# Attention units in three stages one unit apart, with TensorE's order as written, in a two-layer diffusion backbone

## The chip, the core and the metric

The kernel runs on one core of a Trainium2 chip. The core has a matrix engine, TensorE (PE in the rows, with its weight loads as PEld), VectorE (DVE), ScalarE (ACT), GpSimd (POOL) and SyncE (SP), which here mostly issues DMAs. Each engine works through its own queue in order, and engines wait for each other by semaphores. The metric is the device time of one execution in microseconds (us), the median of several runs.

## The reference

Two layers run over 1024 latent tokens (a grid 64 wide) and 256 context tokens, with a width of 1024. A layer projects its input once and gives the columns to three mixers, an mLSTM, a neighbourhood attention and an RG-LRU. Their outputs are concatenated, go through one output projection and are added to the stream; a normed, gated MLP follows. The change concerns the neighbourhood attention and the output projection, which the reference writes so:

```python
q_r = lax.dynamic_index_in_dim(qg, r, axis=1, keepdims=False)
k_band = lax.dynamic_slice_in_dim(kg, sr, wr, axis=1)
...
s_loc = jnp.einsum('bqhd,brqchd->bhqrc', q_r, k_win).astype(jnp.float32) * scale
...
s_loc = (s_loc + bias.astype(jnp.float32)).reshape(b_, NA_HEADS, GRID_W, wr * wc)
s_ctx = jnp.einsum('bqhd,bkhd->bhqk', q_r, kc).astype(jnp.float32) * scale
p = jax.nn.softmax(jnp.concatenate([s_loc, s_ctx], axis=-1), axis=-1).astype(v.dtype)
...
o = jnp.einsum('bhqrc,brqchd->bqhd', p_loc, v_win) + jnp.einsum('bhqk,bkhd->bqhd', p_ctx, vc)
...
x = x + g1[:, None] * (jnp.concatenate([ym, yn, yl], axis=-1) @ w_out)
```

There are 8 heads of 64 columns. A latent token reads a window of 8 by 16 neighbours and all the context; a context token (in layer 0 only) reads the context.

## The kernel before

**Units.** Attention is done in head pairs (`hp`, four of them), and in each pair in units of 128 query tokens: 8 units over latent tokens in either layer, and in layer 0 two over context tokens ahead of them, 40 and 32 units in all. A unit has three parts. *Scores*: QS (the queries) times KH and KL (the keys' high and low part in the matmul's short format) for both heads `e`, into three banks `psa` of PSUM (one for a context unit). VectorE then adds a bias table and takes the maximum (two operations a head), and ScalarE takes the exponential into S and sums the rows into `den`. *Transposes*: S is transposed by TensorE in three groups, called T1, T2 and T3 here (four blocks of the first head, four of the second, and the last block of both); ScalarE copies T1 and T3 and VectorE T2 into PT. *Values*: `den` is inverted, spread to 128 columns as `rb` and transposed into bank `psc`, where PT times the values VB (window) and VC (context) is accumulated too. The result goes to `yr`, scaled by the inverse.

**Prep.** The stacks QS, KH and KL of a head pair are made by `na_prep`, in 6 steps (layer 0) or 5 (layer 1). A step loads `ut`, scales it by VectorE and transposes it into a bank; then for each of the two heads ScalarE copies the high part (KH or QS) and VectorE subtracts it to give the low part (KL or `ql`). The prep of the next head pair runs among the units of this one, a step at a unit's side.

**Fill.** Half of the output projection (its first four row blocks) is done during attention too: chains of 12 matmuls in the one bank `psp`, each with its own read of the stream `xs` and write back, 24 chains in layer 0 and 16 in layer 1. `side()` is called in every unit between scores and transposes; it issues the next prep step and as many chains as are due.

**Banks.** `psa` has three banks, `psb` two, and `psc`, `psp` and `psq` one each. Prep steps (of head pairs 1 to 3) and the three groups of transposes take theirs in the turn b, b, q:

```python
t = bank("bbq")
```

**Order.** The kernel is built with a scheduler that goes over each engine's instructions with a timeline of its own and sets the order of each queue. So the order in which the code issues units, prep steps and chains is not the order on the engines; waits between tiles are kept. Pools give out buffers in turn, so that a tile with `bufs=1` can be loaded again only when its last reader is done.

The functions that the change touches stand here, with the line numbers that the rows use.

Of the kernel before, what the change touches and what calls it, by code (L numbers as in the profile page):

```python
# [11 lines left out]
F32 = mybir.dt.float32  # L12
# [9 lines left out]
P = 128  # L22
# [3 lines left out]
NCTX = 256  # L26
# [65 lines left out]
def backbone_kernel(ctx: ExitStack, tc: tile.TileContext, I, out, dbg=None):  # L92
    nc = tc.nc
    dbg = dbg if dbg is not None else {}
    pe, dve, act, pool, sp = nc.tensor, nc.vector, nc.scalar, nc.gpsimd, nc.sync
# [519 lines left out]
    for l in range(DEPTH):  # L615
# [99 lines left out]
        def softmax_pv(npl, S, den, tiles, vals, permT, ydst):  # L715
# [7 lines left out]
            for gi, gr in enumerate(groups):  # L723
# [37 lines left out]
        anchors = []  # L761

        def new_den():
            return sm.tile([P, 2], F32, name=nm("den"), tag="den", bufs=4)
        def na_att(hp, npl, stacks, yr, side):
# [3 lines left out]
            VC = npl.tile([P, 2, P], F32, name=nm("VC"), tag="VC", bufs=1)  # L769
            uv = u_nv[l]  # L770
            sp.dma_start(VC, uv[0:NCTX, hp * P:(hp + 1) * P].rearrange("(t p) c -> p t c", p=P))

            if not last:
                for qt in range(2):
                    tS = bank("a")
                    S = []
                    den = new_den()
                    for e in range(2):
                        for i, K_ in enumerate((KH, KL)):
                            anchor = pe.matmul(tS[:, e * 256:(e + 1) * 256], QS[e][:, qt * P:(qt + 1) * P],  # L780
                                               K_[e][:, 0:256], start=(i == 0), stop=(i == 1))
                    anchors.append(anchor.ins)
                    for e in range(2):
                        s_ = npl.tile([P, 640], F32, name=nm("S"), tag="S", bufs=4)
                        nmx = sm.tile([P, 1], F32, name=nm("nmx"), tag="nmx", bufs=4)
                        mx = sm.tile([P, 1], F32, name=nm("mx"), tag="mx", bufs=4)
                        sv = tS[:, e * 256:(e + 1) * 256]
                        dve.tensor_reduce(mx, sv, axis=AX.X, op=OP.max)
                        dve.tensor_scalar(nmx, mx, -1.0, None, op0=OP.mult)
                        act.activation(s_[:, :256], sv, AF.Exp, bias=nmx, accum_out=den[:, e:e + 1])  # L790
                        S.append(s_)
# [5 lines left out]
                    side()  # L797
                    phase(f"na_att{l}")
                    softmax_pv(npl, S, den, [(0, P), (P, P)], [VC[:, 0], VC[:, 1]], ident, yd)


            for ct, bs in enumerate(((0,), (1, 2), (3,))):
# [10 lines left out]
                for b in bs:  # L813
                    VB = npl.tile([P, 4, P], F32, name=nm("VB"), tag="VB", bufs=3)
# [6 lines left out]
                    for g in range(2):  # L821
                        nr = 11 if g == 0 else 12
                        nl = nr * 32
                        r0 = 0 if g == 0 else 4
                        kc = (0, 8, 24, 32)[b]
                        qo = NCTX + (1 - g) * 512 + (3 - b) * P
                        tC = bank("a")
                        tL = []
                        for e in range(2):
                            tl = bank("a")  # L830
                            tL.append(tl)
                            for i, K_ in enumerate((KH, KL)):
                                kv = K_[e][:, NCTX:].rearrange("p (r c) -> p r c", c=64)[:, r0:r0 + nr, kc:kc + 32]
                                pe.matmul(tl[:, :nl].rearrange("p (r c) -> p r c", c=32), QS[e][:, qo:qo + P], kv,  # L834
                                          start=(i == 0), stop=(i == 1))
                        for e in range(2):
                            for i, K_ in enumerate((KH, KL)):
                                anchor = pe.matmul(tC[:, e * 256:(e + 1) * 256], QS[e][:, qo:qo + P],
                                                   K_[e][:, 0:256], start=(i == 0), stop=(i == 1))
                        anchors.append(anchor.ins)  # L840
                        S = []
                        den = new_den()
                        for e in range(2):

                            s_ = npl.tile([P, 640], F32, name=nm("S"), tag="S", bufs=4)
                            m1_ = sm.tile([P, 1], F32, name=nm("m1"), tag="m1", bufs=4)
                            m2_ = sm.tile([P, 1], F32, name=nm("m2"), tag="m2", bufs=4)
                            dve.tensor_tensor_reduce(out=s_[:, 0:nl], in0=tL[e][:, :nl],
                                                     in1=tab[e][:, 1 - g, 0:nl],
# [745 lines left out]
```

## Time and profile before

| What | Time |
|---|---|
| median of 3 runs | 3132.05 us (3132.0 to 3132.32) |
| profiled execution | 3124.27 us |
| its span, first to last instruction | 3122.5 us |
| TensorE busy in the span | 3020.2 us, 97% |
| VectorE busy | 1900.0 us, 61% |
| ScalarE busy | 1128.4 us, 36% |
| chain that ended last | PE 70%, DVE 11%, DMA 10% |

All rows come from one profiled execution, 7.8 us below the runs' median. Busy shares count instructions in flight on an engine. The chain that ended last is followed back from the last instruction, at each step to what released it; its shares say on which engine that chain's time was spent. Attention lies at about 510 to 760 us (layer 0) and 2129 to 2350 us (layer 1), with some matmuls of the stage behind it among the last units.

### The profile page before, as it was taken

How to read it: one execution, taken by the hardware profiler on the slowest of the kernel's cores; microseconds unless marked ns; L12 is line 12 of the kernel's file. 1: busy time of each engine (PE TensorE's matmuls, PEld its weight loads, DVE VectorE, ACT ScalarE, POOL GpSimd, SP SyncE). 2: the span in 40 equal slices, each digit the busy share in tenths (PEclk: the TensorE clock that was granted, in tenths of full speed). 3: DMA queues.
4: the chain of work that ended last, by engine and by line, in shares of the span. 5: the costliest groups of instructions: out<-in, count | busy, mean ns of one | idle time of the engine just before them, and what ended most of it. 6: DMA issues, size and time to landing. Idle time of an engine off the chain costs nothing.

```text
span 3122.5 us, 47474 instructions
## 1 busy us (share of the span) xinstructions
PE 3020.2 (97%) x18250; PEld 2558.1 (82%) x18250; DVE 1900.0 (61%) x4318; ACT 1128.4 (36%) x2011; POOL 291.0 (9%) x252
## 2 busy tenths in 40 slices
PE   7999998999899999999999999998899999999999
PEld 6888898778788888887778889997787777887877
DVE  5757655787977667455444574765787444444444
ACT  4632223574421222233222453234564222332222
POOL 0410000222200000010000511002222000000000
PEclk8999999999999999999999999999999999999999
DMA  9624567765233444233323632347753332333233
GB/s 272 216 73 144 171 190 199 226 169 178 68 115 105 126 124 125 75 108 101 95 88 94 175 123 82 100 131 219 219 172 110 95 95 89 99 116 91 92 96 93
DMA packets 531098, 410.73 MB, mean 132 GB/s; under 512 B 27580, under 2 KB 496536, under 8 KB 530872
## 3 DMA queue, kind: packets, MB, share of 16 engines
q1 hardware_dynamic: 519448, 387.41, 41.9%
q0 software_dynamic: 8576, 15.00, 1.5%
q10 hardware_dynamic: 2848, 5.28, 0.5%
q8 instruction: 144, 2.36, 0.3%
q14 instruction: 82, 0.67, 0.1%
HBM read 339.72 MB, written 67.53 MB: 130 GB/s over the span
## 4 chain that ended last, share of the span: by engine, by line
PE 70%; DVE 11%; DMA 10%; issue 2%; ACT 2%; SPq 1%; POOL 0%; ACTq 0%; DVEq 0%; POOLq 0%
PE psa L468 14%; PE psa L1515 13%; PE psq L468 5%; PE psp L468 5%; PE psp L1515 4%; DMA mr<-in_w_mod_dram 4%; PE psq L1515 4%; PE psp L483 4%; PE psq L483 3%; PE psp L1363 3%; DVE ma L344 3%; PE psc L757 2%; PE psb L727 1%; PE psa L1363 1%; PE psa L834 1%
## 5 line engine op out<-in xcount | busy, mean ns | idle before, releaser
L200 ACT ACTIVATE wh<-wr 128x1024 fp32r<-128x1024 f32 (+3 forms) x356 | 361.8, 1021 | 929.7 <-PE psa L1515 296.3
L201 DVE TENSOR_TENSOR wl<-wr,wh 128x1024 fp32r<-128x1024 f32 (+3 forms) x356 | 424.5, 1196 | 380.6 <-ACT wh L200 374.3
L468 PE MATMUL psa<-xlo,wh 128*128 128x512 f32 (+1 forms) x856 | 319.5, 373 | 2.2 <-DVE xlo L444 2.1
L468 PE MATMUL psa<-xh,wh 128*128 128x512 f32 (+1 forms) x856 | 318.8, 373 | 2.4 <-ACT xh L443 2.4
L468 PE MATMUL psa<-xh,wl 128*128 128x512 f32 (+1 forms) x856 | 319.3, 373 | 1.4 <-DVE wl L201 1.4
L1515 PE MATMUL psa<-hl,wh 128*128 128x512 f32 (+1 forms) x768 | 286.1, 373 | 1.3 <-DVE hl L211 1.3
L1515 PE MATMUL psa<-hh,wh 128*128 128x512 f32 (+1 forms) x768 | 284.6, 376 | 0.6 <-ACT wh L200 0.5
L1515 PE MATMUL psa<-hh,wl 128*128 128x512 f32 (+1 forms) x768 | 278.1, 373 | 0.6 <-DVE wl L201 0.6
L1519 DVE SCALAR_TENSOR_TENSOR res<-psa,modt,res 128x512 f32<-128x512 f32 (+1 forms) x192 | 130.9, 693 | 165.8 <-PE psa L1515 165.6
L468 PEld LDWEIGHTS psa<-xlo,wh 128*128 128x128 f32 x856 | 161.6, 189 | 33.4 <-DVE xlo L444 2.9
L468 PEld LDWEIGHTS psa<-xh,wh 128*128 128x128 f32 x856 | 161.5, 189 | 33.4 <-ACT xh L443 2.8
L468 PEld LDWEIGHTS psa<-xh,wl 128*128 128x128 f32 x856 | 161.6, 189 | 32.5 <-DVE wl L201 2.2
L409 POOL TENSOR_TENSOR acc<-acc,nsq 128x512 f32<-128x512 f32 (+1 forms) x56 | 80.3, 1446 | 1020.6 <-ACT nsq L408 970.7
L210 ACT ACTIVATE hh<-rl 128x512 fp32r<-128x512 f32 (+1 forms) x160 | 93.5, 589 | 225.0 <-DVE rl L1491 225.0
L1515 PEld LDWEIGHTS psa<-hh,wh 128*128 128x128 f32 x768 | 144.5, 188 | 34.8 <-ACT wh L200 8.9
L483 PE MATMUL psp<-wl,xh 128*128 128x256 f32 (+1 forms) x560 | 163.1, 291 | 5.9 <-DVE wl L201 5.8
L1515 PEld LDWEIGHTS psa<-hh,wl 128*128 128x128 f32 x768 | 144.5, 188 | 28.6 <-DVE wl L201 1.5
L1515 PEld LDWEIGHTS psa<-hl,wh 128*128 128x128 f32 x768 | 144.6, 188 | 27.8 <-DVE hl L211 1.5
L483 PE MATMUL psp<-wh,xh 128*128 128x256 f32 (+1 forms) x560 | 162.2, 290 | 2.5 <-ACT wh L200 2.4
L483 PE MATMUL psq<-wh,xh 128*128 128x256 f32 (+1 forms) x560 | 162.7, 290 | 1.4 <-ACT usq L641 0.8
L483 PE MATMUL psq<-wl,xh 128*128 128x256 f32 (+1 forms) x560 | 160.9, 287 | 0.0
L483 PE MATMUL psq<-wh,xlo 128*128 128x256 f32 (+1 forms) x560 | 160.2, 286 | 0.0
(409 smaller groups left out, 7342.4 us busy)
## 6 DMA issues: line engine op xcount, KB each, us to landing
wr<-in_w_mlp_dram SPq DMA_DIRECT2D x256, 512.0 KB
mr<-in_w_mod_dram SPq DMA_DIRECT2D x92, 512.0 KB
wr<-in_w_in_dram SPq DMA_DIRECT2D x48, 512.0 KB
tab<-T_d SPq DMA_DIRECT2D x48, 384.0 KB
T_d<-E_d POOLq DMA_DIRECT2D x48, 256.0 KB, 6.5
ab<-row_d SPq DMA_DIRECT2D x36, 256.0 KB
xT_d<-res SPq DMA_DIRECT2D x4, 2048.0 KB
wr<-in_w_out_dram SPq DMA_DIRECT2D x32, 256.0 KB
```

The lines of the kernel that those rows point to most:

```text
L200: act.activation(hi[:, a:b], raw[:, a:b], AF.Copy)
L201: dve.tensor_sub(lo[:, a:b], raw[:, a:b], hi[:, a:b].bitcast(F32))
L210: act.activation(hi, src32, AF.Copy)
L344: dve.scalar_tensor_tensor(a, raw[:, k], s[:, k], a, op0=OP.mult, op1=OP.add)
L409: pool.tensor_add(acc[bi], acc[bi], sq[:, :n])
L468: m = pe.matmul(t[:, :n], w[a][:, k, :], X[bi][b][:, k, :], start=(i == 0), stop=(i == 23))
L483: m = pe.matmul(t[:, :cols], X[bi][b][:, half * 4 + k, o:o + P], ws[half][a][:, k, :], start=(i == 0), stop=(i == 23))
L727: pe.transpose(t[:w, j * P:(j + 1) * P], S[e][:, o:o + w], permT)
L757: pe.matmul(to[64 * e:64 * e + 64, :P], vals[i][:w, 64 * e:64 * e + 64], PT[:w, e, i], start=(i == 0), stop=(i == nt - 1))
L1363: pe.matmul(t[:, :n], w[a][:, k, cc * P:(cc + 1) * P], Y[bi][b][:, k], start=(i == 0), stop=(i == 11))
L1515: m = pe.matmul(t[:, :n], w[a][:, k, cc * P:(cc + 1) * P], H[bi, k][b], start=(i == 0), stop=(i == 3 * GH - 1))
L1519: dve.scalar_tensor_tensor(xr[bi][:, ct], t[:, :n], G2[:, ct, v:v + 1], xr[bi][:, ct], op0=OP.mult, op1=OP.add)
```

## The change

Each unit is now an object of three functions, `scores`, `turn_` (transposes) and `values`. A loop over all units of the four head pairs issues in one iteration the scores of unit u, a slot of fill, a prep step, the transposes of unit u-1, the values of unit u-2, and another slot. A slot issues four matmuls of a projection chain, which now yields after 4 and 8 of its 12 products (the bank `psp` is held meanwhile); between the two parts of the projection four slots stay empty (`LAG`). In this stretch TensorE's instructions are pinned: `keep_in_program_order` keeps them in the order of the code, while the scheduler still orders all other engines. The reciprocal is taken of the spread `den` directly, one operation of 128x128 for two. Buffers: VC 1 to 2, VB 3 to 2, xs 3 to 2, and `yr` in turn from two pools.

```diff
+    pinned = [False]
+    def in_order(op):
+        def issue(*a, **k):
+            ins = op(*a, **k)
+            return tc.keep_in_program_order(ins) if pinned[0] else ins
+        return issue
+    pe = SimpleNamespace(matmul=in_order(nc.tensor.matmul), transpose=in_order(nc.tensor.transpose))
...
-            dve.reciprocal(den, den)
             rb_ = npl.tile([P, 2, 64], F32, name=nm("rb"), tag="rb", bufs=2)
-            dve.tensor_copy(rb_, den.unsqueeze(2).to_broadcast([P, 2, 64]))
+            dve.reciprocal(rb_, den.unsqueeze(2).to_broadcast([P, 2, 64]))
...
-            VC = npl.tile([P, 2, P], F32, name=nm("VC"), tag="VC", bufs=1)
+            VC = npl.tile([P, 2, P], F32, name=nm("VC"), tag="VC", bufs=2)
...
-                    VB = npl.tile([P, 4, P], F32, name=nm("VB"), tag="VB", bufs=3)
+                    VB = npl.tile([P, 4, P], F32, name=nm("VB"), tag="VB", bufs=2)
...
+                                if not wide and i in (4, 8):
+                                    yield
...
-                xs = yp.tile([P, 512], F32, name=nm("xs"), tag="xs", bufs=3)
+                xs = yp.tile([P, 512], F32, name=nm("xs"), tag="xs", bufs=2)
...
+                    for _ in range(LAG if n_ else 0):
+                        yield
...
-            for hp in range(4):
-                def side():
-                    phase(f"na_prep{l}")
-                    if 0 <= hp < 3:
-                        for _ in range(1):
-                            next(preps[hp + 1], None)
-                    for _ in range(due("fill")):
...
+            pinned[0] = True
+            one = two = None
+            for u in itertools.chain(all_units(), (None, None)):
+                if u:
+                    u[0]()
+                slot_()
+                next(side_[0], None)
+                if one:
+                    one[1]()
+                if two:
+                    two[2]()
+                slot_()
+                one, two = u, one
...
+            pinned[0] = False
```

Three places show how the instructions move; in their rows the names are tiles, out<-in, with a number for each tile. The first is TensorE in layer 0, at the last prep step of one head pair (transposes of `ut` into `psq`). Before, the scheduler's order was:

```order
L692 MATMUL psq_7909<-idj,ut_7906 128x2x4x16 x4
L753 MATMUL psc_7763<-idj,rb_7761 128x128
L757 MATMUL psc_7763<-PT_7743,VB_7606 64x128 x6
L757 MATMUL psc_7763<-PT_7743,VC_7474 64x128 x4
L838 MATMUL psa_7960<-KH_6705,QS_6703 128x256
L838 MATMUL psa_7960<-KL_6707,QS_6703 128x256
L838 MATMUL psa_7960<-KH_6706,QS_6704 128x256
L838 MATMUL psa_7960<-KL_6708,QS_6704 128x256
L727 MATMUL psb_7861<-idj,S_7800 128x128
L727 MATMUL psb_7861<-idj,S_7806 128x128
L727 MATMUL psb_7922<-idj,S_7894 128x128 x4
```

In the changed kernel all of TensorE's rows carry the line of the wrapper, L102; the same prep step stands so:

```order
L102 MATMUL psq_7848<-idj,ut_7845 128x2x4x16 x4
L102 MATMUL psb_7861<-idj,S_7744 128x128 x2
L102 MATMUL psb_7861<-idj,S_7744 96x128
L102 MATMUL psb_7861<-idj,S_7744 128x128
L102 MATMUL psb_7869<-idj,S_7750 128x128 x2
L102 MATMUL psb_7869<-idj,S_7750 96x128
L102 MATMUL psb_7869<-idj,S_7750 128x128
L102 MATMUL psq_7877<-idj,S_7744 128x128
L102 MATMUL psq_7877<-idj,S_7750 128x128
L102 MATMUL psc_7883<-idj,rb_7881 128x128
L102 MATMUL psc_7883<-PT_7776,VB_7566 64x128 x6
L102 MATMUL psc_7883<-PT_7776,VC_7419 64x128 x4
```

Before, values (`psc`), scores (`psa`) and transposes into `psb` follow the prep step, and the next user of `psq` comes only 26 rows later. Now T1, T2 (into the two `psb`) and T3 (into `psq`) of one unit follow it, and then the values of the unit before.

The second place is VectorE in layer 1, at a prep step that makes `ql`. Before:

```order
L749 RECIPROCAL den_21922<-den_21922 128x2
L866 TENSOR_TENSOR yr_21618<-yr_21618,psc_21808 128x8x16
L706 SCALAR_TENSOR_TENSOR ql_21943<-psq_21938,gq_17263,QS_21656 64x512
L701 TENSOR_TENSOR KL_21661<-psb_21860,KH_21659 64x512
L751 COPY rb_21985<-den_21922 128x128
L706 SCALAR_TENSOR_TENSOR ql_21943<-psq_21938,gq_17263,QS_21657 64x512
L1380 SCALAR_TENSOR_TENSOR xs_22642<-psp_22629,modt_120,xs_22642 128x512
```

After:

```order
L760 COPY PT_22542<-psb_22551 128x256
L760 COPY PT_22542<-psb_22551 96x128
L760 COPY PT_22542<-psb_22551 128x128
L695 TENSOR_TENSOR ut_22949<-ut_22949,rsn_21471 128x256
L717 SCALAR_TENSOR_TENSOR ql_22535<-psb_22530,gq_17223,QS_22266 64x512
L769 RECIPROCAL rb_22725<-den_22506 128x128
L717 SCALAR_TENSOR_TENSOR ql_22535<-psb_22530,gq_17223,QS_22267 64x512
L909 TENSOR_TENSOR yr_22228<-yr_22228,psc_22565 128x8x16
```

The RECIPROCAL of two columns and the COPY to 128 have become one RECIPROCAL of 128 columns, which here stands between the two `ql` of one bank, where before a COPY of `rb` and a KL stood.

The third place is TensorE where the attention of layer 1 starts: the last transposes of head pair 0's prep and the first scores. Before:

```order
L1363 MATMUL psp_21950<-yh_21746,wh_21765 128x512
L1363 MATMUL psp_21950<-yh_21747,wh_21765 128x512
L1363 MATMUL psp_21950<-yh_21746,wl_21766 128x512
L692 MATMUL psb_21586<-idj,ut_21583 128x2x4x16 x4
L834 MATMUL psa_21633<-KH_21526,QS_21524 128x352
L834 MATMUL psa_21633<-KL_21528,QS_21524 128x352
```

After:

```order
L102 MATMUL psq_21424<-wh_21167,xlo_17191 128x256
L102 MATMUL psb_21515<-idj,ut_21512 128x128 x4
L102 MATMUL psb_21531<-idj,ut_21528 128x2x4x16 x4
L102 MATMUL psb_21546<-idj,ut_21543 128x2x4x16 x4
L102 MATMUL psa_21593<-KH_21486,QS_21484 128x352
L102 MATMUL psa_21593<-KL_21488,QS_21484 128x352
```

Before, 24 matmuls of the fill (L1363, `psp`) stood between the prep of head pair 0 and the first scores (its last three are shown); now none does, and the prep steps and scores follow one another.

## Rows read from the trace of the kernel before

**Rows 1.** Page, part 1: busy us of each engine, share of the span, instructions.

```profile
PE 3020.2 (97%) x18250; PEld 2558.1 (82%) x18250; DVE 1900.0 (61%) x4318; ACT 1128.4 (36%) x2011; POOL 291.0 (9%) x252
```

**Rows 2.** Windows: start:end, length, busy us (count) per engine, TensorE clock, DMA share, GB/s.

```profile
510.00:526.00 16.00, 11.23 (x51) 9.23 (x49) 11.94 (x25) 8.06 (x18) 3.60 (x2) 0.68 0.88 246
526.00:704.00 178.00, 161.95 (x1333) 137.16 (x1332) 140.35 (x450) 109.18 (x283) 38.19 (x20) 0.97 0.72 201
704.00:760.00 56.00, 56.00 (x450) 48.05 (x449) 37.47 (x115) 30.10 (x78) 4.08 (x3) 1.00 0.54 182
2129.00:2148.00 19.00, 12.62 (x50) 9.46 (x49) 10.23 (x12) 5.60 (x9) 13.77 (x8) 0.82 0.95 229
2148.00:2311.00 163.00, 147.63 (x1181) 120.58 (x1180) 133.84 (x409) 98.50 (x246) 40.34 (x22) 0.98 0.75 218
2311.00:2350.00 39.00, 39.00 (x328) 32.54 (x328) 26.42 (x90) 24.52 (x62) 1.61 (x1) 1.00 0.50 170
```

**Rows 3.** Waits of PE, layer 0's body: us in total, times, longest.

```profile
...
PE psc L757 <- DMA VC<-u_nv: 2.4, 2, 2.2
...
PE psb L694 <- DVE KL L701: 2.1, 1, 2.1
...
```

**Rows 4.** Waits of PE, layer 1's body.

```profile
...
PE psa L834 <- DVE m L848: 3.8, 3, 1.7
...
```

**Rows 5.** Timeline of PE, three units without fill products: start, us, instruction.

```profile
...
2313.90 0.41 PE L834 MATMUL psa<-KH,QS 128*128 128x352 f32 x1
...
2321.49 0.60 PE L727 MATMUL psq<-idj,S 128*128 128x128 f32 x4
...
2321.93 0.38 PE L727 MATMUL psb<-idj,S 128*128 128x128 f32 x2
...
2325.80 0.43 PE L834 MATMUL psa<-KH,QS 128*128 128x384 f32 x1
...
```

**Rows 6.** Groups by form, DVE, 510 to 760 us: busy us, mean ns, idle.

```profile
...
L706 DVE SCALAR_TENSOR_TENSOR ql<-psb,gq,QS 64x512 fp32r<-64x512 f32 x12 | 8.8, 746 | 1.2 <-ACT QS L705 1.0
...
L746 DVE COPY PT<-psb 128x512 f32<-128x512 f32 x12 | 8.2, 686 | 1.8 <-PE psc L757 1.1 <-PE psb L727 0.7
...
```

**Rows 7.** Groups by form, ACT, 510 to 760 us.

```profile
...
L855 ACT ACTIVATE S<-S,m 128x640 f32<-128x640 f32 x32 | 26.3, 824 | 12.7 <-DVE m L852 12.7
...
L705 ACT ACTIVATE QS<-psb,gq 64x512 fp32r<-64x512 f32 x12 | 8.0, 679 | 4.4 <-DVE ql L706 2.7 <-PE psb L692 1.7
...
L744 ACT ACTIVATE PT<-psb 128x256 f32<-128x256 f32 x8 | 3.1, 384 | 8.3 <-PE psb L727 8.3
...
L744 ACT ACTIVATE PT<-psb 128x128 f32<-128x128 f32 x8 | 2.2, 276 | 0.0
...
```

**Rows 8.** Timeline around one prep step of layer 0.

```profile
...
563.03 0.66 PE L692 MATMUL psb<-idj,ut 128*128 128x128 f32 x4
...
567.98 0.76 DVE L706 SCALAR_TENSOR_TENSOR ql<-psb,gq,QS 64x512 fp32r<-64x512 f32 x1
...
```

**Rows 9.** Groups by form, DVE, whole span.

```profile
...
L751 DVE COPY rb<-den 128x128 f32<-128x128 f32 x72 | 29.3, 406 | 6.1 <-PE psc L753 4.7
...
L749 DVE RECIPROCAL den<-den 128x2 f32<-128x2 f32 x72 | 11.3, 157 | 9.2 <-ACT S L855 6.1 <-ACT S L790 2.9
...
L1286 DVE RECIPROCAL rc<-dn 128x4 f32<-128x4 f32 x36 | 6.1, 174 | 0.9
...
L168 DVE TENSOR_SCALAR ry<-ri 128x4 int32<-128x4 int32 x8 | 1.3, 166 | 0.1
...
L168 DVE TENSOR_SCALAR rsn<-si 128x40 int32<-128x40 int32 x6 | 0.9, 175 | 0.0
...
```

**Rows 10.** Timeline of PE, start of attention in layer 1.

```profile
...
2144.89 0.40 PE L834 MATMUL psa<-KH,QS 128*128 128x352 f32 x1 [1.24 <-DMA QS<-ql]
...
2146.70 0.63 PE L1363 MATMUL psp<-yh,wh 128*128 128x512 f32 x2
...
2147.39 0.63 PE L1363 MATMUL psp<-yh,wh 128*128 128x512 f32 x2
...
```

More of the change, by code (lines that the diff above doesn't have):

```diff
@@ L1 @@
+import itertools
 import math
@@ L759, in softmax_pv, with na_units, unit, scores @@
             ydst(to[:, :P], to[:, P:2 * P])
[L761 to L765, printed above, removed]
+        def na_units(hp, npl, stacks, yr):
             QS, KH, KL = stacks
-            VC = npl.tile([P, 2, P], F32, name=nm("VC"), tag="VC", bufs=1)
+            VC = npl.tile([P, 2, P], F32, name=nm("VC"), tag="VC", bufs=2)
             uv = u_nv[l]
             sp.dma_start(VC, uv[0:NCTX, hp * P:(hp + 1) * P].rearrange("(t p) c -> p t c", p=P))
+            def unit(score, tiles, vals, permT, yd, end):
+                st = SimpleNamespace()
+                def scores():
+                    st.S, st.den = score()
+                def turn_():
+                    st.PT = transpose_p(npl, st.S, tiles, permT)
+                def values():
+                    values_p(npl, st.PT, st.den, tiles, vals, permT, yd)
+                    if end:
+                        end()
+                return scores, turn_, values
+            def store():
+                if hp == 3:
+                    return
+                y0 = 512 + hp * P
+                if not last:
+                    sp.dma_start(yT_d[l][y0:y0 + P, 0:768], yr[:, 0:768])
+                else:
+                    sp.dma_start(yT_d[l][y0:y0 + P, NCTX:768], yr[:, NCTX:768])
+                sp.dma_start(yT_d[l][y0:y0 + P, 768:], yr[:, 768:])
@@ L773, in na_att @@
             if not last:
                 for qt in range(2):
[L775 to L782, printed above, removed]
@@ L823, in na_att @@
                         nl = nr * 32
[L824 to L835, printed above, removed]
@@ L866, in yd @@
                             dve.tensor_mul(dst, dst, r.rearrange("p (r c) -> p r c", r=8))
[L868 to L878 removed]
+                        yield unit(score, tiles, vals, flip, yd, store if (b, g) == (3, 1) else None)
         with tc.tile_pool(name=f"m1_{l}", bufs=1, reuse_waits="tile") as m1:
@@ L1383, in fill @@
             def fill():
-                for part in parts:
+                for n_, part in enumerate(parts):
                     phase(f"oproj{l}")
@@ L1392, in fill, with slot_ @@
                         phase(f"oproj{l}")
+            LAG = 4
             filler = fill()
-            n_side = 4 * (8 if last else 10)
-            pace = {"fill": sum(8 * len(p_) for p_ in parts), "mod": len(modq), "at": 0}
-            def due(key):
-                i = pace["at"]
-                return (i + 1) * pace[key] // n_side - i * pace[key] // n_side
+            n_slots = 2 * 4 * (8 if last else 10)
+            n_fill = sum(24 * len(p_) for p_ in parts) + LAG
+            at = [0]
+            def slot_():
+                i = at[0]
+                at[0] += 1
+                for _ in range(min(i + 1, n_slots) * n_fill // n_slots - min(i, n_slots) * n_fill // n_slots):
+                    next(filler, None)
             crm = [npl.tile([P, 768], F32, name=nm("crm"), tag="crm", bufs=3) for _ in range(3)]
```

131 lines of the change are left out of this document (72 added, 59 removed).

## The prediction

> **What bounds the kernel now.** I read the page's busy shares first. TensorE (PE) is busy 3020.2 of 3122.5 us, VectorE (DVE) 1900.0 [rows 1]: the kernel can win only PE idle time, 102 us in all, or work on PE. The change adds and removes no matmul, so I looked for the part of the idle time that lies where the order changes. That is attention, about 510 to 760 us in layer 0 and 2129 to 2350 us in layer 1. The stretches [rows 2] show idle time as length less PE busy: layer 0 has 16.00 - 11.23 = 4.8 us at the start, 178 - 161.95 = 16.0 us in the body, none after 704 us. Layer 1 has 19 - 12.62 = 6.4, 163 - 147.63 = 15.4 and none after 2311. So **31.4 us** of idle time stand in the two bodies, and 11.2 us in the two starts. The granted clock averages 0.97 and 0.98 in the bodies. A stretch at the lower of the two clock levels counts one half, so 0.03 x 178 = 5.3 us and 0.02 x 163 = 3.3 us of PE's time are lost there, **8.6 us**. The most that the change can gain in the bodies is therefore 40 us, 1.3%.
>
> Then the waits. In layer 0's body PE waits for the copy of the context values VC (2.4 us, two times) and for the second VectorE half of a key stack, KL, which holds a psb bank (2.1 us) [rows 3]. In layer 1 the largest is the score reduction that frees psa (3.8 us in three) [rows 4]. They are many small waits on different things; no one resource sets the end.
>
> **What the change takes away.** VC gets two buffers: 2.4 us of the 31.4. The rest of the gain comes from the three stages. Between the scores of a unit and its transposes now lies one iteration of other PE work, and again between the transposes and the values, so the softmax chain (reductions, exponential, copies of PT) is covered. I allow it everything: **-31.4 us**. I do not count the clock loss as gained, since new waits follow.
>
> **What it adds: waits for a PSUM bank.** An iteration with a prep step needs four banks for transposes: one for the prep step, then T1, T2 and T3 (S transposed to PT). There are three: two psb and psq. The scheduler of before set other work between two users of one bank: in the PE piece of layer 0 above, scores and values follow the prep transposes. In the new order T1, T2 and T3 follow at once, and the third of them takes the bank that the prep step filled; PE has only the eight transposes of T1 and T2 in between. Four transposes take 2321.93 - 2321.49 = 0.44 us [rows 5], so 0.88 us. Emptying a prep bank is a chain of four: QS on ScalarE (ACT) 0.68, ql on DVE 0.75, and both again for the other head [rows 6, 7], 2.85 us with nothing else in either queue. A case of before shows how it goes among other work: transposes from 563.03 to 563.03 + 4 x 0.11 = 563.47, last ql over at 567.98 + 0.76 = 568.74, so 5.3 us [rows 8]. Following each bank through the order of the changed kernel I find two sorts of such waits, 25 that matter:
> - 8 (4 in each layer) in which T3 waits for the prep bank. At least 2.85 - 0.88 = 2.0 us, at most, with the 5.3 us of the trace, 4.4. I take 3.0, one longer instruction in the way (an exponential is 0.82 us [rows 7]): 8 x 3.0 = 24 us (16 to 35).
> - 17 (7 and 10) in which T2 or T3 takes the bank of an earlier T of the same unit, with 0.44 us of PE work between them where ACT empties it (0.38 + 0.28 us for its two copies [rows 7]) and none where DVE does (0.69 us [rows 6]). Alone that is 0.2 to 0.7 us, 0.45 in the mean. I take one longer instruction ahead of the copy, +1.0 us: 1.45 x 17 = 25 us (8 with a free queue; 17 x 2.6 = 44 with an instruction of 1.0 to 1.2 us ahead in both).
>
> Together **+49 us** (24 to 79). What waits behind: the T3, the values, the four fill products and the next scores all stand behind the stopped transpose, since PE's order is pinned. Before, the scheduler had placed fill work at these places. I take the middle because VectorE's queue is fuller:
>
> **The merged reciprocal.** A unit had a RECIPROCAL of 128x2 (157 ns) and a COPY that spreads it to 128x128 (406 ns in the mean); now one RECIPROCAL of 128x128. The trace has no such size. Two elements cost 157 ns, four 174, so 8.5 ns for an element more, where a TENSOR_SCALAR of 40 elements takes hardly longer than one of 4 (175 to 166) [rows 9]. Carried on, 157 + 126 x 8.5 = 1.23 us. From below: an operation of that size at the copy's price, 0.41. I take 1.23, since the slope is this operation's own. Net +0.67 us of DVE a unit, +27 us on 40 units and +21 us on 32, beside 190 us that DVE is busy in 250 us of layer 0 and 170 in 221 of layer 1 (sums of [rows 2]). DVE comes to 217 and 191 us, close to PE's 229 and 199. Not a bound by itself, but in the DVE piece above, the reciprocal stands between the first and the second ql of one prep bank, and there adds its 1.2 us to the wait for the bank. The rows' slope has a counterpart in the Trainium skill ("VectorE: DVE Perf Modes", section "First, the fixed hardware budget"): Reciprocal is an iterative divide with a repeat count of 8. By that and the page's clock of 0.96 GHz I estimate 8.3 ns an element, 1.1 us for 128; the sum would be the same.
>
> **The start.** Before, scores wait for the copy of QS (the first of layer 1 starts at 2144.89, after 1.24 us of waiting [rows 10]), and fill products run ahead of them: 24 512-column products in layer 1. In the new order none stand before those scores, so 24 x 0.23 us (2147.39 - 2146.70 for three [rows 10]) = 5.6 us of work comes later; in layer 0 the order has 12 fewer ahead of the first scores of a latent unit, narrower ones among them, about 2 us. Against it, the weight splits for this fill no longer stand in ACT's and DVE's queues ahead of QS and ql, so scores may begin sooner. From 0 to 7.6 us: **+4**.
>
> **The rest at nothing.** VB and xs lose one of three buffers: both are loaded an iteration or more ahead (a unit takes 11.9 / 3 = 4.0 us of PE time without fill [rows 5]); if not, a load's wait comes into each second pair of units. The projection in steps of four and LAG are the same matmuls; yr alternates between two pools, as its two halves did.
>
> Sum: -31.4 + 49 + 4 = **+21 us**. The profiled execution took 3124.27 us, so 3145; the runs' median is 7.8 us above it, 3132.05, and the forecast for a median is **3153**.
>
> **Rivals.**
> - *Faster.* The bank waits come to their floor, 24 us, with the start at 0 and the clock's 8.6 us won back, because longer gaps that cost the clock are gone: -31.4 + 24 - 8.6 = -16, 3116. For it: the schedule of ACT and DVE was made anew against the pinned order and may put each emptying copy first. Against: the DVE piece shows a reciprocal between two ql. It decides at 49 - 21 = 28 us for all 25 waits, 1.1 us each.
> - *Cancelled.* A reciprocal at the copy's price (then DVE does less than before), or waits of 25 to 32 us: within 6 us of 3132.
> - *Longer.* Each emptying behind two long instructions, 79 us: +52, 3184. The nearest row, 5.3 us, speaks for it; that fill work no longer competes for ACT speaks against it.
> - *The clock.* Short stops come at almost every prep iteration, 33 of them. In the bodies of before the clock fell with 31 us of idle time [rows 2]; if the stops double the loss, 8.6 us more: +30, 3162. In the Trainium skill ("TensorE: Matmul & The Clock Gate", section "A second HAM failure mode: psum-queue depth-cycling") such short stops between groups of matmuls on cycling banks make the clock swing; no row here shows it.
>
> **How the numbers follow.** Measurement tells 0.2% (6.3 us) from no change. The likeliest case and the clock together 0.47 (own range 3139 to 3175), longer 0.09, cancelled 0.16, faster 0.28. So slower 0.56, same 0.16, faster 0.28. To leave out no more than 2 in 10, the range reaches from 3116, the faster rival's own time, to 3184, the longer one's.
>
> **What would show it.** After: RECIPROCAL 128x128 x72 at 1.1 to 1.3 us, no COPY of rb; PE waits for psb and psq with ql, KL or PT as releasers summing to 25 to 80 us, in the first five or six units of head pairs 0 to 2; hardly any wait of values for PT or VC; and head pair 3, which has no prep, dense. It would be wrong if these waits stay under 1 us each, if the reciprocal takes 0.4 us, or if the scores wait for psa behind DVE (then longer).

## The result: 3209 us, 2.5% slower, and the profile after

The changed kernel takes 3209.14 us (median of 4 runs, 3206.58 to 3212.07) where the kernel before takes 3132.03; the ratio is 1.0248, with a 95% interval from 1.0230 to 1.0266. The sign was forecast, the size was not: 77 us against 21, and outside the range (3116 to 3184).

The page of the changed kernel, part 1, answers to [rows 1]:

```profile
PE 3036.4 (95%) x18250; PEld 2576.0 (80%) x18250; DVE 1931.4 (60%) x4246; ACT 1127.7 (35%) x2011; POOL 282.0 (9%) x252
```

The span grew from 3122.5 to 3204.8 us, by 82.3. PE is busy 16.2 us longer with the same 18250 matmuls, which the clock can account for (worked out in the section on why the prediction was wrong), and idle 168.4 us in place of 102.3. So 66 us are new idle time. The windows (columns as in [rows 2]) show where; the stretches are the start, the head pairs with prep beside them, and the end, in layer 0 and layer 1:

```profile
510.00:541.00 31.00, 17.23 (x92) 14.75 (x91) 21.52 (x49) 14.93 (x32) 7.22 (x4) 0.78 0.94 243
541.00:705.00 164.00, 125.87 (x983) 108.11 (x981) 115.80 (x309) 81.25 (x212) 25.77 (x14) 0.89 0.56 159
705.00:790.00 85.00, 84.36 (x709) 72.81 (x708) 63.70 (x181) 46.27 (x127) 11.84 (x6) 0.99 0.47 145
2170.00:2200.00 30.00, 8.61 (x33) 5.94 (x32) 11.86 (x23) 6.68 (x13) 17.07 (x10) 0.59 0.99 223
2200.00:2360.00 160.00, 127.36 (x932) 107.42 (x933) 114.80 (x301) 80.83 (x199) 25.77 (x14) 0.89 0.58 160
2360.00:2429.00 69.00, 68.96 (x578) 59.25 (x577) 52.83 (x152) 37.78 (x103) 10.91 (x6) 1.00 0.58 182
```

Where prep runs, PE is idle 164 - 125.87 = 38 us in layer 0 and 160 - 127.36 = 33 in layer 1, at a granted clock of 0.89 (0.97 and 0.98 in [rows 2]). Where it does not, PE is busy without a gap: the three stages as such run dense. The starts are idle 13.8 and 21.4 us. The largest waits in the two starts (us in total, times, longest), the first in layer 0, the others in layer 1:

```profile
PE psb L102 <- DVE ql L717: 9.3, 1, 9.3
...
PE psa L102 <- DMA VB<-u_nv: 7.9, 1, 7.9
PE psb L102 <- DVE KL L712: 6.4, 1, 6.4
PE psa L102 <- DVE m L889: 4.7, 2, 3.8
```

The two on `psb` are prep transposes, the two on `psa` scores. A score does not read VB; the row names the transfer that landed last, and QS's copy was issued 2.1 us before that score began, so which of the two held it is not told.

Which waits these are stands in the groups by form of PE: transposes of S (T1 to T3) and of `ut` (prep) by bank, and behind the second bar the idle time before them and what ended it. The changed kernel:

```profile
L102 PE MATMUL psb<-idj,S 128*128 128x128 f32 x400 | 67.4, 283 | 24.3 <-DVE PT L760 14.3 <-ACT PT L758 5.6 <-DVE KL L712 2.4
L102 PE MATMUL psq<-idj,S 128*128 128x128 f32 x208 | 39.3, 290 | 38.4 <-DVE ql L717 25.4 <-DVE KL L712 12.9
L102 PE MATMUL psb<-idj,ut 128*128 128x128 f32 x114 | 19.9, 298 | 17.2 <-DVE ql L717 9.3 <-DVE KL L712 6.4 <-DVE ut L695 1.4
L102 PE MATMUL psq<-idj,ut 128*128 128x128 f32 x38 | 6.7, 297 | 1.1 <-DVE ut L695 1.1
```

and the same groups in the kernel before, where the transposes of `ut` stand at two lines:

```profile
L727 PE MATMUL psb<-idj,S 128*128 128x128 f32 x400 | 71.2, 282 | 4.3 <-DVE PT L746 1.0 <-ACT S L855 0.9 <-DVE ql L706 0.8
L727 PE MATMUL psq<-idj,S 128*128 128x128 f32 x208 | 37.9, 279 | 1.8 <-DVE ql L706 0.9 <-DVE KL L701 0.4 <-ACT S L855 0.3
L694 PE MATMUL psb<-idj,ut 128*128 128x128 f32 x66 | 10.9, 278 | 3.3 <-DVE KL L701 2.1 <-DVE ut L684 1.1
L692 PE MATMUL psb<-idj,ut 128*128 128x128 f32 x48 | 7.4, 276 | 0.4 <-DVE KL L701 0.4
L694 PE MATMUL psq<-idj,ut 128*128 128x128 f32 x22 | 3.8, 286 | 0.2 <-ACT S L855 0.2
L692 PE MATMUL psq<-idj,ut 128*128 128x128 f32 x16 | 2.5, 278 | 1.1 <-DVE ut L684 1.1
```

T1 to T3 wait 62.7 us in place of 6.1, all of it in the stretches with prep, and prep transposes 18.3 in place of 5.0. All that T1 to T3 wait for at psq is the emptying of a prep bank (ql, KL), nine times, 4.3 us each in the mean. One of these waits, of 6.25 us, in the timeline of the changed kernel, DVE, PE and SP's queue (a time in brackets is the idle time before, and its releaser):

```profile
540.36 0.38 PE L102 MATMUL psq<-idj,ut 128*128 128x128 f32 x2
...
540.57 1.04 PE L102 MATMUL psb<-idj,S 128*128 128x128 f32 x8
540.76 0.36 SPq L692 DMA_DIRECT2D ut<-u_nq  x1
...
541.87 0.81 DVE L760 COPY PT<-psb 128x256 f32<-128x256 f32 x3
...
542.60 0.47 DVE L717 SCALAR_TENSOR_TENSOR ql<-psq,gq,QS 64x256 fp32r<-64x256 f32 x1
...
546.50 0.69 DVE L695 TENSOR_TENSOR ut<-ut,rsn 128x512 f32<-128x512 f32 x1 [3.44 <-DMA ut<-u_nq]
547.22 0.49 DVE L717 SCALAR_TENSOR_TENSOR ql<-psq,gq,QS 64x256 fp32r<-64x256 f32 x1
...
547.86 0.66 PE L102 MATMUL psq<-idj,S 128*128 128x128 f32 x2 [6.25 <-DVE ql L717]
```

Two prep transposes fill psq, eight transposes of S follow into psb, and T3 wants psq. The first `ql` is done at 543.07. The second stands in VectorE's queue behind the scaling of the *next* step's `ut`, whose load was issued only at 540.76, once the prep transposes had read the buffer; VectorE stands idle 3.44 us until it lands. T3, the values, the fill and the next scores stand behind that.

Not all of the nine are like this. In only one other does VectorE stand idle for more than 1 us in front of a `ut` (2.77 us of a wait of 6.36), and over all nine it is some 8 us of the 38.4. In the wait at the last prep step of layer 0, ordinary work stands in the way:

```profile
697.31 0.60 PE L102 MATMUL psq<-idj,ut 128*128 128x128 f32 x4
...
699.04 1.65 ACT L221 ACTIVATE yh<-yl 128x512 fp32r<-128x512 f32 x3
...
700.60 0.81 ACT L896 ACTIVATE S<-S,m 128x640 f32<-128x640 f32 x1
...
701.42 0.66 ACT L716 ACTIVATE QS<-psq,gq 64x512 fp32r<-64x512 f32 x1
...
703.61 0.76 DVE L717 SCALAR_TENSOR_TENSOR ql<-psq,gq,QS 64x512 fp32r<-64x512 f32 x1 [0.75 <-ACT QS L716]
704.51 0.66 PE L102 MATMUL psq<-idj,S 128*128 128x128 f32 x2 [5.73 <-DVE ql L717]
```

Three copies of the fill's input (`yh`) and an exponential run on ScalarE ahead of the first QS, and no load is waited for.

The merged reciprocal, in the groups by form of DVE, answers to the first two of [rows 9]:

```profile
L769 DVE RECIPROCAL rb<-den 128x128 f32<-128x128 f32 x72 | 68.3, 949 | 32.9 <-ACT S L896 22.7 <-PE psc L102 6.5 <-ACT S L831 2.1
```

### The profile page after: what moved, and what is told of

It is laid out like the page before. It is cut to its first block, busy times and chain, and to the rows that moved or that the text cites. A ratio compares the mean times of both kernels' runs of the same rounds, so it can differ in the third digit from the quotient of the medians.

```text
span 3204.8 us, 47458 instructions
## 1 busy us (share of the span) xinstructions
PE 3036.4 (95%) x18250; PEld 2576.0 (80%) x18250; DVE 1931.4 (60%) x4246; ACT 1127.7 (35%) x2011; POOL 282.0 (9%) x252
## 4 chain that ended last, share of the span: by engine, by line
PE 69%; DVE 11%; DMA 10%; ACT 2%; issue 2%; SPq 1%; ACTq 0%; DVEq 0%
PE psa L102 31%; PE psp L102 16%; PE psq L102 14%; PE psb L102 5%; DMA mr<-in_w_mod_dram 4%; PE psc L102 3%; DVE ma L355 3%; DMA ut<-u_nk 1%; DMA ut<-u_nq 1%; DMA ab<-row_d 1%; DVE wl L212 1%; DMA yT_d<-ysb 1%; DMA yl<-yT_d 0%; DVE res L1568 0%; DVE hl L222 0%
## 5 line engine op out<-in xcount | busy, mean ns | idle before, releaser
L102 PE MATMUL psa<-xlo,wh 128*128 128x512 f32 (+1 forms) x972 | 361.5, 372 | 1.7 <-DVE xlo L455 1.7
L102 PE MATMUL psa<-xh,wl 128*128 128x512 f32 (+1 forms) x972 | 360.4, 372 | 2.6 <-DVE wl L212 2.6
L102 PE MATMUL psa<-xh,wh 128*128 128x512 f32 (+1 forms) x972 | 360.4, 373 | 1.2 <-ACT wh L211 0.7
L102 PE MATMUL psa<-hl,wh 128*128 128x512 f32 (+1 forms) x768 | 286.0, 373 | 0.6 <-DVE hl L222 0.6
L102 PE MATMUL psa<-hh,wh 128*128 128x512 f32 (+1 forms) x768 | 284.7, 376 | 0.3 <-ACT wh L211 0.3
L102 PE MATMUL psa<-hh,wl 128*128 128x512 f32 (+1 forms) x768 | 278.3, 373 | 0.6 <-DVE wl L212 0.6
L102 PEld LDWEIGHTS psa<-xlo,wh 128*128 128x128 f32 x972 | 183.8, 189 | 37.5 <-DVE xlo L455 2.3
L102 PEld LDWEIGHTS psa<-xh,wl 128*128 128x128 f32 x972 | 183.4, 189 | 37.7 <-DVE wl L212 3.8
L102 PEld LDWEIGHTS psa<-xh,wh 128*128 128x128 f32 x972 | 183.5, 189 | 36.6 <-ACT wh L211 1.4
L102 PEld LDWEIGHTS psa<-hh,wh 128*128 128x128 f32 x768 | 144.3, 188 | 34.8 <-ACT wh L211 8.6
L102 PE MATMUL psp<-wl,xh 128*128 128x256 f32 (+1 forms) x560 | 162.3, 290 | 6.3 <-DVE wl L212 6.2
L102 PEld LDWEIGHTS psa<-hh,wl 128*128 128x128 f32 x768 | 144.4, 188 | 28.8 <-DVE wl L212 1.5
L102 PEld LDWEIGHTS psa<-hl,wh 128*128 128x128 f32 x768 | 144.5, 188 | 27.4 <-DVE hl L222 0.8
L102 PE MATMUL psp<-wh,xh 128*128 128x256 f32 (+1 forms) x560 | 161.8, 289 | 3.8 <-ACT wh L211 2.4
L102 PE MATMUL psq<-wh,xh 128*128 128x256 f32 (+1 forms) x560 | 161.7, 289 | 2.5 <-ACT usq L652 1.3
L102 PE MATMUL psq<-wl,xh 128*128 128x256 f32 (+1 forms) x560 | 159.9, 286 | 0.0
L102 PE MATMUL psq<-wh,xlo 128*128 128x256 f32 (+1 forms) x560 | 159.2, 284 | 0.0
```

Source lines behind the costliest of these rows:

```text
L102: ins = op(*a, **k)
```

## Experiments

All ratios are to the kernel before on the same chip, with 95% intervals; the changed kernel is 1.0248. Differences in us are between medians of different sessions, in which the kernel before lay between 3132.0 and 3135.3 us, so they are good to a few us. Each edit is made in the changed kernel unless said otherwise.

**e1, TensorE's order left to the scheduler.**

```diff
-            pinned[0] = True
+            pinned[0] = False
```

> The changed kernel with its TensorE order left to the scheduler; all else stays (three stages, steps of four, buffers, merged reciprocal). Theory A (the pinned order makes transposes wait for banks, 62 us of waits, and the clock falls in them): most of the 77 us goes, 3120 to 3150 us. Rival B (the buffers, the loads and the fuller VectorE queue are to blame, not the order): it stays above 3180 us.

3140.09 us, ratio 1.0013 (1.0002 to 1.0024). Theory A held and B fell: with all else of the change in place, the order as pinned is what costs some 70 us. The transposes of S wait little again:

```profile
L102 PE MATMUL psb<-idj,S 128*128 128x128 f32 x400 | 68.7, 280 | 6.8 <-ACT S L896 2.5 <-DVE ql L717 2.4 <-DVE m L893 0.9
L102 PE MATMUL psq<-idj,S 128*128 128x128 f32 x208 | 38.5, 280 | 1.5 <-DVE m L893 0.9 <-DVE ql L717 0.4
```

**e2, the prep step behind the values, order pinned.**

```diff
-                phase(f"na_prep{l}")
-                next(side_[0], None)
-                phase(f"na_att{l}")
                 if one:
                     one[1]()
                 if two:
                     two[2]()
+                phase(f"na_prep{l}")
+                next(side_[0], None)
+                phase(f"na_att{l}")
```

> The changed kernel with the prep step moved behind the values of its iteration, TensorE's order still pinned. Between the prep transposes and the next user of their bank then lie two slots of fill, the scores and two groups of transposes, some 4 us in place of 0.9. Theory A: the T3 waits (38 us in nine) and the stops at the start (15 us of prep transposes that wait for a bank) go nearly all, the clock comes back in part: 3140 to 3165 us. Rival B (VectorE is late whatever the order): the waits move to other tiles, above 3190 us.

3171.75 us, ratio 1.0118 (1.0100 to 1.0137), 37 us less than the changed kernel. The place of the prep step is worth half of the loss, a little less than A had it. The psq waits fall from 38.4 to 21.0 us, and PE's busy time is back at 3019.8:

```profile
L102 PE MATMUL psb<-idj,S 128*128 128x128 f32 x400 | 65.8, 279 | 18.3 <-DVE PT L760 5.3 <-DVE ql L717 4.3 <-ACT PT L758 4.1
L102 PE MATMUL psq<-idj,S 128*128 128x128 f32 x208 | 37.5, 280 | 21.0 <-DVE ql L717 13.5 <-DVE KL L712 5.5 <-DVE PT L760 1.6
```

```profile
PE 3019.8 (95%) x18250; PEld 2562.7 (81%) x18250; DVE 1928.8 (61%) x4246; ACT 1129.4 (36%) x2011; POOL 281.4 (9%) x252
```

The prep transposes still wait, 21.0 us where the changed kernel has 18.3, so that part of the expectation was wrong.

**e3, three buffers for `ut`.**

```diff
-                    ut = npl.tile([P, 4, P], F32, name=nm("ut"), tag="ut", bufs=2)
+                    ut = npl.tile([P, 4, P], F32, name=nm("ut"), tag="ut", bufs=3)
...
-                    yl_ = tp.tile([P, 512], F32, name=nm("yl"), tag="nsq", bufs=3)
+                    yl_ = tp.tile([P, 512], F32, name=nm("yl"), tag="nsq", bufs=3 if tp is yk else 2)
```

> The changed kernel with three buffers for ut, the loaded tile of a prep step, in place of two (paid for by two in place of three for the tile yl in the load of the fill's input). Theory A1 (the bank is emptied late because in VectorE's queue the scaling of the next ut, which waits for its load, stands ahead of ql or KL): the T3 waits fall to about half, 3165 to 3185 us. Rival (the bank is late because of the queues' ordinary work): within 8 us of 3209.

3216.54 us, ratio 1.0254 (1.0233 to 1.0276): no gain. But it didn't take the suspected wait away. VectorE stands 28.3 + 27.3 = 56 us ahead of the scaling, against 62 in the changed kernel (rows below e5): the scheduler made VectorE's queue anew, and the scaling met late loads again (4.24 us at 557.54 us). So it is no test of A1. It does show that a bank is emptied late without a late load too: in a T3 wait of 4.68 us, ending at 551.44 us, VectorE stood idle 0.58 us for a load.

```profile
L695 DVE TENSOR_TENSOR ut<-ut,rsn 128x512 f32<-128x512 f32 x32 | 24.9, 780 | 28.3 <-DMA ut<-u_nq 15.1 <-DMA ut<-u_nk 13.0
L695 DVE TENSOR_TENSOR ut<-ut,rsn 128x256 f32<-128x256 f32 x12 | 6.9, 571 | 27.3 <-DMA ut<-u_nk 21.5 <-DMA ut<-u_nq 5.7
```

**e4, the reciprocal of two columns and the copy.**

```diff
-            dve.reciprocal(rb_, den.unsqueeze(2).to_broadcast([P, 2, 64]))
+            dve.reciprocal(den, den)
+            dve.tensor_copy(rb_, den.unsqueeze(2).to_broadcast([P, 2, 64]))
```

> The changed kernel with the reciprocal of two columns and the copy to 128 in place of the one reciprocal of 128 columns (949 ns in the trace, 157 and about 230 to 410 before). Theory C (the longer reciprocal between two subtractions of one bank lengthens the waits): 25 waits of up to 0.5 us less and VectorE 28 us less busy, 3190 to 3200 us. Rival (it lies beside other waits): within 5 us of 3209.

3205.24 us, ratio 1.0227 (1.0210 to 1.0244): 4 us less, and the intervals overlap. It lies beside other waits here, as the rival said, and theory C is not borne out. VectorE is busy 1906.3 us, 25 less.

**e5, `ut`'s scaling behind the last KL or ql on VectorE.** `low[0]` is the last subtraction of a prep step, and `issue_after` sets the order in the queue.

```diff
+        low = [None]
...
-                    dve.tensor_mul(uv, uv, rsn[kd, grp][:, a:b, h0:h0 + 2].unsqueeze(3).to_broadcast([P, n, 2, 64]))
+                    with (tc.issue_after(low[0].ins) if low[0] is not None and hp else nullcontext()):
+                        dve.tensor_mul(uv, uv, rsn[kd, grp][:, a:b, h0:h0 + 2].unsqueeze(3).to_broadcast([P, n, 2, 64]))
...
-                            dve.tensor_sub(KL[e][own[e], cs], t[own[e], :w], KH[e][own[e], cs].bitcast(F32))
+                            low[0] = dve.tensor_sub(KL[e][own[e], cs], t[own[e], :w], KH[e][own[e], cs].bitcast(F32))
...
```

(`ql`'s subtraction is kept in `low[0]` in the same way.)

> The changed kernel with one constraint on VectorE's queue: the scaling of a prep step's ut comes behind the last KL or ql of the step before. Theory A1 (VectorE stands at the scaling, which waits for its load, with the ql or KL behind it that would free the bank: 3.4 us in one case of the changed kernel's trace): VectorE no longer stands in front of ql, the nine T3 waits fall from 38 us to about 20, and the time to 3175 to 3195 us. Rival (the emptying is late by ordinary work in the queues): within 8 us of 3209.

3181.6 us, ratio 1.0146 (1.0113 to 1.0179), 28 us less: A1 held for that part. VectorE's standing at the scaling, in the changed kernel

```profile
L695 DVE TENSOR_TENSOR ut<-ut,rsn 128x512 f32<-128x512 f32 x32 | 22.6, 708 | 35.2 <-DMA ut<-u_nk 17.9 <-DMA ut<-u_nq 17.2
L695 DVE TENSOR_TENSOR ut<-ut,rsn 128x256 f32<-128x256 f32 x12 | 5.5, 455 | 26.9 <-DMA ut<-u_nk 22.1 <-DMA ut<-u_nq 4.8
```

falls from 62.1 us to 20.0 in e5, and the psq waits from 38.4 to 26.8, not quite to the 20 expected:

```profile
L698 DVE TENSOR_TENSOR ut<-ut,rsn 128x512 f32<-128x512 f32 x32 | 29.3, 915 | 5.4 <-DMA ut<-u_nq 3.0 <-DMA ut<-u_nk 1.5
L698 DVE TENSOR_TENSOR ut<-ut,rsn 128x256 f32<-128x256 f32 x12 | 5.1, 426 | 14.6 <-DMA ut<-u_nk 13.1 <-DMA ut<-u_nq 1.2
```

```profile
L102 PE MATMUL psq<-idj,S 128*128 128x128 f32 x208 | 38.5, 286 | 26.8 <-DVE ql L720 18.9 <-DVE KL L715 8.0
```

**e6, prep from a head pair's third unit.**

```diff
-                next(side_[0], None)
+                if at[0] // 2 % (8 if last else 10) >= 2:
+                    next(side_[0], None)
```

> The changed kernel with a head pair's prep steps begun at its third unit and not at its first. Theory D (at the start of each layer the prep step of the next head pair waits for a bank that the prep of the first one still holds, and all scores stand behind it): the 15 us of prep transposes that wait and some of the scores' 18 us go, 3185 to 3197 us. Rival (the starts are bound by the copies of the stacks, whatever the prep does): within 8 us of 3209.

3236.54 us, ratio 1.0320 (1.0289 to 1.0351), 27 us more. Theory D fell, and the time went further than its rival said: the prep transposes do wait less, 9.6 us in place of 18.3, but the time is longer. In the order as pinned, other steps and other units come together, and T1 to T3 wait 83.7 us; what makes this phase worse than the other was not followed up.

```profile
L102 PE MATMUL psb<-idj,S 128*128 128x128 f32 x400 | 67.3, 281 | 37.6 <-DVE PT L760 17.5 <-ACT PT L758 15.1 <-DVE ql L717 3.0
L102 PE MATMUL psq<-idj,S 128*128 128x128 f32 x208 | 39.4, 291 | 46.1 <-DVE KL L712 23.2 <-DVE ql L717 22.9
```

**e7, the kernel before with the merged reciprocal alone.**

```diff
-            dve.reciprocal(den, den)
             rb_ = npl.tile([P, 2, 64], F32, name=nm("rb"), tag="rb", bufs=2)
-            dve.tensor_copy(rb_, den.unsqueeze(2).to_broadcast([P, 2, 64]))
+            dve.reciprocal(rb_, den.unsqueeze(2).to_broadcast([P, 2, 64]))
```

> The kernel before with the merged reciprocal alone. It adds 949 - 157 - 230 to 406 ns, 0.4 to 0.55 us, to VectorE in each of 72 units, 28 to 40 us in all. Theory (TensorE is the bound, and the scheduler can place other work meanwhile): within 5 us of the kernel before. Rival (VectorE lies on the path in the units with prep): 5 to 15 us slower.

3140.95 us, ratio 1.0019 (1.0005 to 1.0032): some 6 us, slower beyond the interval. That is at the lower end of the rival's 5 to 15 us, but the interval, 2 to 10 us, reaches into both expectations.

**e8, e10 and e13, the edits together, order pinned.** e8 is e2, e4, e5 and e6 together; e10 leaves e6 out; e13 leaves e4 out as well, so that it is e2 and e5 alone.

> The changed kernel with TensorE's order still pinned, and four edits together: prep behind the values, prep from the third unit, ut's scaling behind the last KL or ql, reciprocal of two columns and copy. Theory A (bank waits, at the start and in the body, make the loss): near the unpinned kernel, 3130 to 3150 us. Rival (a pinned order loses by every late DMA whatever stands in it): above 3155 us.

("The combined kernel of before" in the next expectation is e8.)

> The combined kernel of before (3152 us) with the prep steps again from a head pair's first unit; so TensorE pinned, prep behind the values, ut's scaling behind the last KL or ql, reciprocal of two columns and copy. If a later prep costs time of its own, as it did alone (+27 us), this is 5 to 15 us faster, 3137 to 3147; if that cost came from the turn of the banks in the old order alone, within 5 us of 3152.

> The changed kernel with the prep steps behind the values and ut's scaling behind the last KL or ql; the merged reciprocal stays. The two alone gave 37 and 28 us, and the old reciprocal 4 on the changed kernel. If the three add, 3209 - 37 - 28 = 3144 us, 5 to 10 above the kernel with the old reciprocal (3136). If the reciprocal matters only through the bank waits, within 5 us of 3136.

e8: 3151.88 us, ratio 1.0053 (1.0039 to 1.0067), just above the range of theory A and below the rival's. e10: 3136.13 us, ratio 0.9996 (0.9984 to 1.0008), no difference from the kernel before. e13: 3145.44 us, ratio 1.0031 (1.0022 to 1.0040). So the prep's place and the scaling's place add, 37 and 28 us, to the 64 of e13. The reciprocal costs 9 us once most of the bank waits of T1 to T3 are gone (e13 against e10), twice its 4 on the changed kernel, and e6's later start costs 16 here too. A pinned order need not lose: e10 has it. It does not equal the kernel before by having no waits: its prep transposes still wait 23.6 us and PE is idle 117.7 us, 15 more than before, but PE is busy 13 us less. Its page, and its waits of T1 to T3, 24.9 us of the 62.7:

```profile
PE 3007.3 (96%) x18250; PEld 2554.6 (82%) x18250; DVE 1911.5 (61%) x4318; ACT 1127.4 (36%) x2011; POOL 283.1 (9%) x252
```

```profile
L102 PE MATMUL psb<-idj,S 128*128 128x128 f32 x400 | 63.9, 276 | 11.1 <-ACT PT L761 4.3 <-DVE ql L720 2.3 <-DVE KL L715 1.8
L102 PE MATMUL psq<-idj,S 128*128 128x128 f32 x208 | 36.6, 275 | 13.8 <-DVE ql L720 10.5 <-DVE KL L715 3.2
```

**e9 and e11, 24 fill products ahead of the first scores**, in the changed kernel and in e10.

```diff
+            for _ in range(6):
+                next(filler, None)
             pinned[0] = True
```

> The changed kernel with the first 24 fill products of each layer issued ahead of the first scores, as the scheduler of before had them. Theory D2 (the starts lose because PE has nothing to do while the stacks of the first head pair are emptied and copied): 24 products of 0.12 to 0.23 us in each layer come out of the body, and the clock is up sooner, 3194 to 3202 us. Rival (more work in ACT's, VectorE's and the DMA queues at the start makes the stacks later by as much): within 5 us of 3209.

> The kernel just above with the 24 fill products of each layer ahead of the first scores. By theories A, A1 and D2 together the waits of the pinned order are back at about those of before: 3125 to 3140 us. Rival (a pinned order pays for every late load): above 3145.

e9: 3206.47 us, ratio 1.0220 (1.0202 to 1.0239), no gain to speak of. e11: 3148.77 us, ratio 1.0040 (1.0026 to 1.0054), 13 us slower than e10. D2 fell in both, and e11 lies in its rival's range, though nothing here shows that late loads are the reason. In e9 the prep transposes no longer wait at the start, 1.5 us where the changed kernel has 17.2, but T1 to T3 wait 80.7 in place of 62.7: the wait moved.

```profile
L102 PE MATMUL psb<-idj,S 128*128 128x128 f32 x400 | 66.7, 281 | 38.8 <-DVE PT L760 12.9 <-DVE KL L712 12.6 <-ACT PT L758 12.5
L102 PE MATMUL psq<-idj,S 128*128 128x128 f32 x208 | 38.6, 285 | 41.9 <-DVE ql L717 24.2 <-DVE KL L712 16.8 <-ACT S L831 0.9
L102 PE MATMUL psb<-idj,ut 128*128 128x128 f32 x114 | 18.2, 280 | 1.5 <-DVE ut L695 1.3 <-PE psa L102 0.2
```

**e12, e14 and e15, where the scheduler orders TensorE.** e12 is e1 and e4 together; e14 is the kernel before with e5's edit; e15 is e12 with it.

> The changed kernel without the pinned order and with the reciprocal of two columns and copy; three stages, steps of four and the buffers stay. The merged reciprocal cost the kernel before 6 us and the unpinned one stood at +4, so if these add, 3128 to 3135 us, no slower than the kernel before. Rival (three stages cost time of their own): 3138 us or more.

> The kernel before with ut's scaling behind the last KL or ql on VectorE. Theory A1 as a cost of the pinned order only (the scheduler gives TensorE other work meanwhile): within 6 us of the kernel before. Rival (VectorE's 32 us of idle time ahead of ut cost the kernel before too): 6 to 15 us faster.

> The changed kernel without the pinned order, with the reciprocal of two columns and copy, and with ut's scaling behind the last KL or ql. Same two theories: within 6 us of the kernel before, or 6 to 15 us faster.

e12: 3135.57 us, ratio 0.9996 (0.9984 to 1.0008). e14: 3144.02, ratio 1.0030 (1.0015 to 1.0045). e15: 3138.07, ratio 1.0014 (1.0000 to 1.0028). Three stages, steps of four and the buffers cost nothing of their own (e12 with the order free, e10 with it pinned). Where TensorE's order is free, VectorE's standing at the scaling costs nothing that the constraint would win back: it is 29.1 + 17.6 = 46.7 us in the kernel before and 47.4 in e12, and 15.0 in e15, which is no faster. In the kernel before the constraint makes it 9 us slower, which neither expectation had. No version was faster than the kernel before beyond the interval, e10 and e12 being its equals.

## Why the prediction was wrong

**The mechanism was right, some of its sizes by luck.** T1 to T3 that wait for a bank were the main term: 8 + 17 waits forecast at 49 us (24 to 79), 62.7 measured. For the 17 the middle was 25 us, and psb measured 24.3. Of these, 14 waits behind copies of PT make 19.9, 1.4 us each as forecast; the other 4.4 are waits of another sort, KL among them, so that the sums agree as they do is luck. For the 8 it was 3.0 us each, 24 in all, and psq measured 38.4 in nine, 4.3 each, at the top of the 2.0 to 4.4 that the prediction gave. This term was mis-sized at "I take 3.0, one longer instruction in the way". More than one stood in the way: in two of the nine VectorE idle in front of the scaling of the next `ut`, behind a load, in others several instructions that run. The prediction's own order rows of VectorE show `ut` directly ahead of `ql`; I priced the reciprocal beside it and read past the one instruction there that waits for a DMA. e5 took 11.6 of the 38.4 us away, and 26.8 stayed. Its 28 us are more than that: between the two profiles the span falls by 22.4, T1 to T3 wait 15.6 less, prep transposes 6.3 more, PE is busy 4.3 less, and 8.8 are other idle time that was not followed up.

**What the change takes away, -31.4 us, and the start, +4, failed most.** Where a start ends is a choice (the windows are 31 and 30 us long, 16 and 19 before), so the two are taken together: -27.4 forecast. Before, attention was idle 31.4 + 11.2 = 42.6 us. After, it is idle 35.2 us in the starts and 70.8 where prep runs; without the 62.7 of T1 to T3, 43.3 are left. So nothing went, where 27.4 should have: 28 of the 61 us that the forecast is short. In the stretches with prep only 8 us of other idle time are left, so "I allow it everything" was nearly right there. The starts are where it failed. In place of fill that comes later, the runs show prep transposes that wait, 16.8 us (9.3 and 6.4 for a bank, 1.1 for `ut`), which no term of the sum had, and scores that wait, 17.7 us, where before fill had waited.

**Why the starts cost this stays open.** The explanation that I gave, fill products that no longer run ahead, fell with e9 and e11: with these products back, the same time was lost at T1 to T3. With prep later (e6) the prep transposes wait half as long and the time is longer; in e10, which equals the kernel before, they wait 23.6 us.

**The clock, at 0 in the sum and 8.6 us in a rival, came to 16.2.** That is PE's busy time, 3036.4 against 3020.2, for the same matmuls. As an estimate, busy time times what the granted clock lacks to 1.00, over the six windows, is 36 us after and 14 before, 22 more, so the clock can account for all of it. The granted clock in the stretches with prep fell from 0.97 and 0.98 to 0.89. It reads 0.50 from 545 to 553 us, in and behind the wait of 6.25 us, and 1.00 from 555 to 587. With fewer stops in the pinned order the busy time is back: e2 has 3019.8, e10 3007.3. The Trainium skill ("TensorE: Matmul & The Clock Gate", section "A second HAM failure mode: psum-queue depth-cycling"), which the prediction weighed, says that such short stops between groups of matmuls on cycling banks make the clock swing between its two levels. The trace agrees: where T1 to T3 stop at banks the granted clock is 0.89 in the mean, so in part at the lower level (1.2 GHz), and right behind these stretches, without stops, 0.99 and 1.00.

So the sum, in the prediction's terms: +0.7 for -27.4, 62.7 for 49, 16.2 for 0, and 2.7 of idle time elsewhere make 82.3 us, the growth of the span. (The prediction's own sum comes to 21.6, not 21, and 24 x 0.23 to 5.5, not 5.6; neither matters.)

**The reciprocal.** I took 1.23 us from the slope of 8.5 ns an element; it took 949 ns, so (949 - 157) / 126 = 6.3 ns an element. A slope from two and four elements was too steep, but nearer than the copy's price. By the Trainium skill ("VectorE: DVE Perf Modes", "First, the fixed hardware budget") the estimate was 1.1 us; the measurement is below that too, and decides. So the sign "1.1 to 1.3 us" did not come. Its effect was small beside the stops (4 us, within the intervals) and 6 to 9 us without them, so "that there adds its 1.2 us to the wait for the bank" was too much.

**VB and xs at nothing** held: e10 and e12, which have both at two buffers, equal the kernel before. **Head pair 3 dense** held as well: 84.36 of 85 and 68.96 of 69 us busy.

**Of the rivals,** none came as written. The bank waits came between the middle and "longer" (62.7 against 49 and 79), "the clock" came at 16 where it had 8.6, and the starts were in none. The probabilities had "longer" and "the clock" apart; with both in the case, the range should have reached past 3190.

## What to carry to other kernels

To pin one engine's order makes it wait for late producers on the other engines: follow each bank or buffer to the instructions that empty it, and count in their engines' queues what stands ahead, both what runs and what waits for a DMA. The second kind can be moved by one constraint, as e5 did, and is easily read past. Bank waits are to be looked for in every user of a bank: here the prep transposes were left out. With the order pinned, the distance in work between two users of a bank is a design number: here it was 0.9 us for an emptying of some 5, and moving one step behind the values was worth 37 us.

## What the runs showed of the hardware that was not expected

A VectorE reciprocal of 128x128 takes 949 ns, one of 128x2 157 and of 128x4 175: it grows with the elements, but less than the small sizes suggest. TensorE's busy time for the same 18250 matmuls ran from 3007.3 us (e10) to 3050.2 (e6), both with TensorE's order pinned. T1 to T3 wait 24.9 us in the one and 83.7 in the other, and the granted clock over the span is 0.990 and 0.975, so there stops went with more than their own length. Stops are not all of it: e1, with the order free, waits 8.3 us there and is busy 3029.1.
